# Value products of two attentions: from two query tiles at a time to four

## The chip, the cores and the metric

The kernel runs on one core of a Trainium2 chip. The metric is the device time of one execution in microseconds (us); of the kernel before there are three such times, and one more execution was taken by the profiler. Lower is better.

## The reference, cut to what matters

Two layers of a bidirectional encoder over 1024 tokens of width 1024, all in float32. Layer 0 is a differential attention with 8 heads (two score matrices a head, and a value width of 128), layer 1 a latent attention with 8 heads (one score matrix a head, value width 128). What the change touches is the last line of each attention block, the product of the probabilities with the values:

```
# layer 0
p = softmax(scores); p = p[:, :, 0] - lam * p[:, :, 1]
o = einsum('bhqk,bkhd->bqhd', p, v)
# layer 1
p = softmax(scores)
o = einsum('bhqk,bkhd->bqhd', p, v)
```

Each head has 1024 queries, 1024 keys and 128 value columns. Before and after the attentions stand the input and output projections, norms and gates.

## The kernel before, in words

**Products in three passes.** An f32 operand is kept as two f32r tiles, a rounded part and the rest, and every product is three matmuls that add up in one PSUM bank (`mm3`, L183 to L186).

**Work of one query tile.** Queries go in tiles of 128, eight to a head. In layer 0 `q_tile` (L763) makes two score tiles of 128x1024 (called c0 and c1 here; four matmuls of 512 columns each). `softmax_part` (L396) takes the negated row maximum on DVE (L399) and the exponential on ACT (L401). The c1 scores are overwritten by their exponentials in PSUM, and the two are combined on DVE (L779 to L781), so the PSUM of c1 comes free only with L781. There are two such PSUM tiles (tag `sc`), used in turn. In layer 1 `scores1` (L1595) makes one score tile with ten matmuls and softmax works on that.

**From scores to output.** A finished tile is a `Tail` (L869). Its `turn(kh)` transposes four 128x128 blocks on TensorE into the one `tr` bank (L382), ACT copies them out as `pth` (L384) and DVE writes the rest `ptl` (L385). Its `pv(kh)` makes 4 x 3 matmuls of a value block with the transposed probabilities, for half of the keys; two calls make the 24 matmuls that one pair of query tiles needs. Two tiles share one set of `pth`/`ptl` (`alloc_pt`, 256 columns), so `pv` does something for every second tile only, with 256 moving columns. The output bank `o_` takes four tiles (one half of the queries); with its second pair it is closed, which starts the norm or gate of that half.

**Order of the work.** `attn0` (L931) and `attn1` (L1618) issue one slot for each query tile: the scores of this tile, `turn(1)` of the tile two back, and then `after_scores` (L914): `turn(0)` of the last tile and `pv` of the tile two back. Between these, `fill(i)` takes some steps of a stream: the input projections (layer 0) or the low-rank expansions (layer 1) that later heads need. A step is one `mm3` of 512 columns into an `acc` bank; eight steps in layer 0 make one half of a strip, whose result goes through rope: an ACT copy, four DMAs, products on POOL and DVE, and DMAs that place the halves of q and k. The tables `FILL0`, `FILL1` and `FILL7` (the last head of layer 0) say how many steps each place of each slot gets. In layer 0 a slot gets 6 steps, in layer 1 two slots get 3 together. Strips bring their weights by DMA (L208), and split them on ACT (L229) and POOL (L230).

**A scheduler** in the language's tile layer then orders the instructions of each engine by its own estimate of what is ready, so the built order can differ from the one written. On SP, where the DMAs are issued, and on the other engines, the order of the built program is kept in the run.

**Values.** The values of a layer are computed in `v0_tile` (L667) and `v1_tile` (L1471), stored to DRAM by `store_v` (L359) and read back for each head by `load_v` (L369) just ahead of that head's first `pv`. Eight of the value tiles of layer 1 use the buffers of `pth` and `ptl` (tag `pt`, six of 128x2x512) before the attention needs these.

Of the kernel before, what the change touches and what calls it, by code (L numbers as in the profile page):

```python
# [12 lines left out]
F32R = mybir.dt.float32r  # L13
# [8 lines left out]
P = 128  # L22
# [63 lines left out]
def trunk(ctx: ExitStack, tc: tile.TileContext, A, out):  # L86
# [96 lines left out]
    def mm3(psum, ah, al, bh, bl, first, last):  # L183
        PE.matmul(psum, ah, bh, start=first, stop=False)  # L184
        PE.matmul(psum, ah, bl, start=False, stop=False)  # L185
        PE.matmul(psum, al, bh, start=False, stop=last)  # L186
# [94 lines left out]
    class Side:  # L281


        def __init__(self):
            self.q = []
# [70 lines left out]
            SP.dma_start(f32v(t[64:128, 0, :]), f32v(t[0:64, 0, :]))  # L356
            SP.dma_start(f32v(t[0:64, 1, :]), f32v(t[64:128, 1, :]))

    def store_v(l, sp, acc, tt, fh, tag="vst", bufs=None):  # L359
        v = sp.tile([P, 2, HF], F32R, name="v_hl", tag=tag, bufs=bufs or VB[l])  # L360
# [16 lines left out]
    def transpose_p(p, pth, ptl, t, kh):  # L377

        tr = bank("tr", "tr", [P, 4, P])
        for j in range(4):  # L380
            kt = kh * 4 + j
            PE.transpose(tr[:, j, :], p[:, kt * P : (kt + 1) * P], ident)  # L382
        dst = slice(t * P, (t + 1) * P)
        mk["S"] = S.copy(pth[kh][:, :, dst], tr).ins  # L384
        mk["V"] = V.tensor_sub(ptl[kh][:, :, dst], tr, f32v(pth[kh][:, :, dst])).ins  # L385
# [483 lines left out]
    class Tail:  # L869


        def __init__(self, qp, t, e, zz, c):
            self.qp, self.t, self.e, self.zz, self.c = qp, t, e, zz, c
            self.mate = tails[1]

        def turn(self, kh):
            if kh == 0:
                self.pt = alloc_pt(self.c["pool"]) if self.t == 0 else self.mate.pt
                self.mate = None
            transpose_p(self.e, *self.pt, self.t, kh)  # L880

        def pv(self, kh):
            c, qp = self.c, self.qp
            if self.t == 0:
                return
            if kh == 0:
                if qp == 0:
                    c["vt"] = load_v(c["pool"], c["l"], c["h"])
                if qp % 2 == 0:
                    c["o_"] = bank("pv", "pv")  # L890
                    c["open"](qp // 2)
            cs = slice((qp % 2) * 256, (qp % 2) * 256 + 256)
            pv(c["o_"][:, cs], c["vt"], *self.pt, kh)
            if kh == 1 and qp % 2 == 1:
                c["close"](qp // 2, c["o_"], self.zz)

    tails, hooks = [None, None], []

    def run_tails(fill):

        prev, last = tails
        prev.turn(1)
        fill(0)
        last.turn(0)
        prev.pv(0)
        prev.pv(1)
        fill(1)
        last.turn(1)
        fill(2)
        last.pv(0)  # L910
        last.pv(1)
        tails[:] = [None, None]

    def after_scores(fill, n):  # L914

        prev, last = tails
        if last:
            last.turn(0)
        fill(n)
        if prev:  # L920
            prev.pv(0)
        fill(n + 1)
        new = hooks[:]
        if prev:
            prev.pv(1)
        fill(n + 2)
        for f in new:
            hooks.remove(f)
            f()

    def attn0(h, fills, extra=None, late=None):  # L931

        def close(half, o_, zz):
            if late and half == 1:
                ctx_["late"] = late(o_, zz)
                return
            o = a0b.tile([P, HF], F32, name="o", tag="o", bufs=2)
            sq = a0b.tile([P, HF], F32, name="osq", tag="osq", bufs=4)
            head_out(o_, o, sq)
            subln(o, sq, zz, half, h, None)  # L940

        ctx_ = dict(pool=a0b, l=0, h=h, open=lambda half: None, close=close)
        for qp in range(4):
            half = qp // 2
            if qp % 2 == 0:
                zz = first.pop(0) if first else sm.tile([P, 4], F32, name="zz")
            for t in range(2):
                fl = fills(qp * 2 + t)

                def fill(i):  # L950
                    if fl[i]:
                        stream0.step(fl[i])

                def mid(c):
                    if c == 0:
                        fill(0)
                        if tails[0]:
# [10 lines left out]
                tails[:] = [tails[1], Tail(qp, t, e0, zz, ctx_)]  # L968
                if extra:
                    extra(qp * 2 + t)  # L970
        if late:
            run_tails(lambda i: extra(8 + i))
            while hooks:
                hooks.pop(0)()
            return ctx_["late"]
# [492 lines left out]
            G.tensor_sub(l_, raw, f32v(h_))  # L1468
            wk[k][fh] = (h_, l_)

    def v1_tile(tt, fh, sp, *buf):  # L1471
# [5 lines left out]
        store_v(1, sp, acc, tt, fh, *buf)  # L1477

    CK, CQ = [[None, None] for _ in range(2)], [[None, None] for _ in range(3)]

# [137 lines left out]
    def attn1(h, fills, extra=None, late=None):  # L1618

        def open_(half):  # L1620
            ctx_["gz"] = wst.tile([P, HF], F32, name="gz1", tag="gz", bufs=3)
            SP.dma_start(ctx_["gz"], zS[h, half])

        def close(half, o_, zz):
            if late and half == 1:
                ctx_["late"] = late(o_, zz, ctx_["gz"])
                return
            o = ap2.tile([P, HF], F32, name="o1", tag="o", bufs=2)
            V.scalar_tensor_tensor(out=o, in0=o_, scalar=0.5, in1=ctx_["gz"], op0=ALU.mult, op1=ALU.mult)
            V.reciprocal(zz, zz)  # L1630
            finish(o, zz, 1, h, half, None, ap2, None)

        ctx_ = dict(pool=ap, l=1, h=h, open=open_, close=close)
        for qp in range(4):
            half = qp // 2
            if qp % 2 == 0:
                zz = first1.pop(0) if first1 else sm.tile([P, 4], F32, name="zz1")
            for t in range(2):
                ti = (qp * 2 + t) % 4
                fl = fills(qp * 2 + t)  # L1640

# [10 lines left out]
                tails[:] = [tails[1], Tail(qp, t, e, zz, ctx_)]  # L1652
                if extra:
                    extra(qp * 2 + t)
        if late:
            run_tails(lambda i: extra(8 + i))
            while hooks:
                hooks.pop(0)()
            return ctx_["late"]

    stream1.step(6)
    v1_left = list(range(NT))
    for n, steps in zip(V1_AT, (steps1[0] - 6, 0)):
        for tt in v1_left[:n]:
            v1_tile(tt, 1, ap, "pt", 6)
        del v1_left[:n]
        stream1.step(steps)
    side.flush()
# [1 line left out]
    zz0 = sm.tile([P, 4], F32, name="zz1")  # L1670
    first1 += [zz0, scores1(0, 0, 0, zz0)]
    for tt in v1_left:
        v1_tile(tt, 1, ap, "pt", 6)
    stv.close()
    ap2 = pool(st5, "attn1b")
    for h in range(NH - 1):
# [166 lines left out]
```

## Time and profile before

| | us |
|---|---|
| median of three executions | 1443.31 |
| lowest and highest | 1442.59 and 1443.35 |
| profiled execution, its own time | 1438.65 |
| its span, first to last instruction | 1436.9 |
| TensorE (PE) busy | 1388.8 |
| PE weight loads busy | 1158.8 |
| VectorE (DVE) busy | 917.5 |
| ScalarE (ACT) busy | 728.7 |
| GpSimd (POOL) busy | 610.6 |

The profiled execution was 4.66 us faster than the median, and 1.75 us of its time lie outside the span. The mean granted clock of TensorE is 0.997.

How to read the rows that follow: a row of a timeline has the start and the duration in us, the engine, the line of the kernel, the operation, output<-inputs, the shape, and a count; in brackets is the idle time of the engine before it and what ended it. A matmul's duration overlaps that of the next, so the cost of one in a dense stream is the distance between two starts. A row of a group has the total busy time and the mean in ns after the bar, and behind the second bar the engine's idle time just before its instructions.

### The profile page before, as it was taken

To read this page: it belongs to the slowest core of one execution; us is meant where nothing else is said; L and a number is where in the kernel's file an instruction comes from. 1 tells how busy PE (TensorE), PEld (TensorE's weight loads), DVE (VectorE), ACT (ScalarE), POOL (GpSimd) and SP (SyncE) were. 2 spreads that over 40 slices of the span, in tenths; PEclk is the share of its full clock that TensorE was granted. 3 is DMA by queue.
4 is the path that set the end of the run, shared out by engine and by line. 5 is a ranking of instruction groups with operands and counts; after the bars stand their busy time and mean duration, and the time that the engine had idled before them with its cause. 6 is when DMAs were issued, how large, how long until landed. Compare 5 with 4: busy or idle time off the path is not lost. (4 is left out here: it accounts for less than half of the span.)

```text
span 1436.9 us, 20644 instructions
## 1 busy us (share of the span) xinstructions
PE 1388.8 (97%) x7388; PEld 1158.8 (81%) x7388; DVE 917.5 (64%) x1372; ACT 728.7 (51%) x1287; POOL 610.6 (42%) x483
## 2 busy tenths in 40 slices
PE   5999999999999999998999999999999999999997
PEld 4778788888888888887787877887888888888886
DVE  6656877767777767677435985545666555555355
ACT  5622375666565656566343452335455554545342
POOL 4416164656464646464461343532141331412572
PEclk9999999999999999999999999999999999999999
DMA  8787723333332333237653145398343432336563
GB/s 326 238 254 237 255 70 93 84 104 81 96 101 84 96 89 91 86 96 248 236 183 125 38 132 184 122 305 236 133 130 111 130 101 77 104 96 217 185 237 136
DMA packets 135527, 213.70 MB, mean 149 GB/s; under 512 B 19072, under 2 KB 56064, under 8 KB 135424
## 3 DMA queue, kind: packets, MB, share of 16 engines
q1 hardware_dynamic: 135424, 212.38, 47.1%
q8 instruction: 58, 0.95, 0.3%
q14 instruction: 45, 0.37, 0.1%
HBM read 137.92 MB, written 50.80 MB: 131 GB/s over the span
## 5 line engine op out<-in xcount | busy, mean ns | idle before, releaser
L384 ACT CAST pth<-tr 128x512 fp32r<-128x512 f32 x256 | 150.6, 588 | 284.2 <-PE tr L382 281.9
L399 DVE TENSOR_REDUCE nm<-s 128x1 f32<-128x1024 f32 x192 | 234.1, 1219 | 77.2 <-PE s L773 65.7
L385 DVE TENSOR_TENSOR ptl<-tr,pth 128x512 fp32r<-128x512 f32 x256 | 176.2, 688 | 139.4 <-ACT pth L384 138.9
L230 POOL TENSOR_TENSOR wl<-wraw,wh 128x512 fp32r<-128x512 f32 (+2 forms) x79 | 103.6, 1314 | 205.6 <-ACT wh L229 183.4
L401 ACT ACTIVATE e<-s,nm 128x1024 f32<-128x1024 f32 x128 | 143.7, 1123 | 29.8 <-DVE nm L399 29.2
L382 PE MATMUL tr<-ident,e 128*128 128x128 f32 x1024 | 155.1, 274 | 2.3 <-DVE ptl L385 2.0
L382 PEld LDWEIGHTS tr<-ident,e 128*128 128x128 f32 x1024 | 121.2, 140 | 43.6 <-DVE ptl L385 19.2
L184 PE MATMUL acc<-h0h,wh 128*128 128x512 f32 x360 | 150.1, 417 | 1.9 <-DVE v_hl L362 1.8
L184 PE MATMUL pv<-pth,vt 128*128 128x256 f32 x512 | 147.1, 287 | 0.0
L185 PE MATMUL pv<-ptl,vt 128*128 128x256 f32 x512 | 145.8, 285 | 0.0
L186 PE MATMUL pv<-pth,vt 128*128 128x256 f32 x512 | 144.7, 283 | 0.0
L186 PE MATMUL acc<-h0h,wl 128*128 128x512 f32 x360 | 143.1, 398 | 0.5 <-POOL wl L230 0.5
L185 PE MATMUL acc<-h0l,wh 128*128 128x512 f32 x360 | 142.0, 394 | 0.0
L1013 POOL TENSOR_TENSOR wol<-wor,woh 128x512 fp32r<-128x512 f32 x64 | 85.0, 1351 | 84.7 <-ACT woh L1012 77.2
L185 PEld LDWEIGHTS pv<-ptl,vt 128*128 128x128 f32 x512 | 97.6, 191 | 2.9
L184 PEld LDWEIGHTS pv<-pth,vt 128*128 128x128 f32 x512 | 97.4, 190 | 2.9 <-ACT pth L384 0.2
L186 PEld LDWEIGHTS pv<-pth,vt 128*128 128x128 f32 x512 | 97.6, 191 | 0.1
L326 POOL TENSOR_TENSOR rp_r<-rp_raw,cosT 128x512 f32<-128x512 f32 x38 | 49.8, 1311 | 91.0 <-ACT rp_raw L321 50.8
L331 POOL TENSOR_TENSOR rp_sw<-rp_sw,sinT 128x512 f32<-128x512 f32 x42 | 55.4, 1318 | 74.1 <-DMA rp_sw<-rp_raw 73.9
L773 PE MATMUL s<-ks,qa 128*128 128x512 f32 x256 | 82.6, 404 | 2.8 <-DVE e L781 2.6
L781 DVE SCALAR_TENSOR_TENSOR e<-s,z,e 128x1024 f32<-128x1024 f32 x64 | 82.1, 1283 | 2.1
L773 PE MATMUL s<-ks,qb 128*128 128x512 f32 x256 | 81.1, 395 | 0.0
(590 smaller groups left out, 3335.4 us busy)
## 6 DMA issues: line engine op xcount, KB each, us to landing
ada<-in_ada_ss SPq DMA_DIRECT2D x32, 512.0 KB, 6.0
wraw<-in_w_s SPq DMA_DIRECT2D x64, 256.0 KB, 2.9
vS<-v_hl SPq DMA_DIRECT2D x32, 512.0 KB, 5.9
vt<-vS SPq DMA_DIRECT2D x32, 512.0 KB, 3.7
wor<-in_w_out SPq DMA_DIRECT2D x64, 256.0 KB, 3.9
rp_sw<-rp_raw SPq DMA_DIRECT2D x168, 64.0 KB, 2.0
bc_s<-bc_d SPq DMA_DIRECT2D x34, 256.0 KB, 4.1
oS<-bc_s SPq DMA_DIRECT2D x30, 256.0 KB, 2.5
```

The lines of the kernel that those rows point to most:

```text
L184: PE.matmul(psum, ah, bh, start=first, stop=False)
L185: PE.matmul(psum, ah, bl, start=False, stop=False)
L186: PE.matmul(psum, al, bh, start=False, stop=last)
L230: sub = (V if pair_of else G).tensor_sub(l_[:, :n], raw[:, :n], f32v(h_[:, :n]))
L382: PE.transpose(tr[:, j, :], p[:, kt * P : (kt + 1) * P], ident)
L384: mk["S"] = S.copy(pth[kh][:, :, dst], tr).ins
L385: mk["V"] = V.tensor_sub(ptl[kh][:, :, dst], tr, f32v(pth[kh][:, :, dst])).ins
L399: mk["V"] = V.reduce_max(nm, s_ps, axis=AX.X, negate=True).ins
L401: mk["S"] = S.activation(e, s_ps, AF.Exp, bias=nm, scale=1.0, accum_out=zs).ins
L773: PE.matmul(s_ps[:, kc * HF : (kc + 1) * HF], src[:, c, ql], KS[h][kc][:, c, :], start=fst, stop=not fst)
L781: combined.append(V.scalar_tensor_tensor(out=e0, in0=e1, scalar=z1[:, 0:1], in1=e0, op0=ALU.mult, op1=ALU.add).ins)
L1013: in_turn(G.tensor_sub(lo, raw, f32v(hi)))
```

## The change

`Tail` now counts tiles 0 to 7 of a head. The transposed probabilities of four tiles (512 columns) go into one set of tiles, and `pv` does its work with the fourth of them: 24 matmuls of 512 columns where there were two times 24 of 256. The second half of the last head of each layer keeps pairs (`pairs`). The tiles of the two key halves have tags of their own (`pt0`, `pt1`), two buffers each, that is one set and no second one: the first tile of the next four can be written when the `pv` of that key half is through. So `pv(0)` now stands ahead of `turn(0)` of the last tile.

The steps of the stream are moved out of the slots with a `pv` (1 and 5): the others get 8 in layer 0 and 2 in layer 1. The sum over a head is the same. The eight value tiles of layer 1 now sit two by two in the four new buffers. Lastly a reserve for DMA descriptors that software writes is set to 1024 bytes, which leaves more of the on-chip memory to the tiles.

```
-FILL0 = ((1, 2, 1, 1, 1, 0), (1, 1, 1, 1, 1, 1)) * 3 + ((1, 2, 1, 1, 1, 0), (1, 1, 1, 1, 1, 0))
-FILL1 = ((1, 0, 1, 0), (0, 1, 0, 0)) * 4
+FILL0 = ((2, 2, 1, 2, 0, 1), (0, 0, 0, 0, 0, 0), (2, 2, 1, 2, 0, 1), (2, 2, 1, 2, 0, 1)) + ((2, 2, 1, 2, 0, 1), (0, 0, 0, 0, 0, 0), (2, 2, 1, 2, 0, 1), (2, 2, 1, 2, 0, 0))
+FILL1 = ((1, 1, 0, 0), (0, 0, 0, 0), (1, 1, 0, 0), (1, 1, 0, 0)) * 2
-FILL7 = ((0, 1, 1, 1, 1, 0),) * 4
+FILL7 = ((1, 1, 1, 2, 0, 0), (0, 0, 0, 0, 0, 0), (1, 1, 1, 2, 0, 0), (1, 1, 1, 3, 0, 0))
...
-    def pv(o_, vt, pth, ptl, kh):
+    def pv(o_, vt, pth, ptl, kh, cs):
         for j in range(4):
-            mm3(o_, vt[kh][:, 0, j, :], vt[kh][:, 1, j, :], pth[kh][:, j, :], ptl[kh][:, j, :], kh + j == 0, kh * 4 + j == NT - 1)
+            mm3(o_[:, cs], vt[kh][:, 0, j, :], vt[kh][:, 1, j, :], pth[kh][:, j, cs], ptl[kh][:, j, cs], kh + j == 0, kh * 4 + j == NT - 1)
...
-    def alloc_pt(ap_):
-        pth = [ap_.tile([P, 4, 2 * P], F32R, name="pth", tag="pt", bufs=6) for _ in range(2)]
-        ptl = [ap_.tile([P, 4, 2 * P], F32R, name="ptl", tag="pt", bufs=6) for _ in range(2)]
-        return pth, ptl
+    def pt_tile(ap_, kh, name):
+        return ap_.tile([P, 4, HF], F32R, name=name, tag=f"pt{kh}", bufs=2)
...
     class Tail:
         def turn(self, kh):
-            if kh == 0:
-                self.pt = alloc_pt(self.c["pool"]) if self.t == 0 else self.mate.pt
-                self.mate = None
-            transpose_p(self.e, *self.pt, self.t, kh)
+            if self.i == 0:
+                for parts, name in zip(self.pt, ("pth", "ptl")):
+                    parts[kh] = pt_tile(self.c["pool"], kh, name)
+            transpose_p(self.e, *self.pt, self.i, kh)
+        def due(self):
+            return self.i == 3 or (self.pairs and self.i == 1)
...
     def after_scores(fill, n):
         prev, last = tails
+        if prev:
+            prev.pv(0)
         if last:
             last.turn(0)
         fill(n)
-        if prev:
-            prev.pv(0)
         fill(n + 1)
...
+    def v1_home(tt):
+        if tt % 2 == 0:
+            v1_bufs.append(pt_tile(ap, (tt // 2) % 2, "v_hl"))
+        return v1_bufs[-1][:, tt % 2 * 2 : tt % 2 * 2 + 2, :]
...
-    nc = bacc.Bacc("TRN2", target_bir_lowering=False, num_devices=1)
+    nc = bacc.Bacc("TRN2", target_bir_lowering=False, num_devices=1, dynamic_dma_scratch_size=1024)
```

More of the change, by code (lines that the diff above doesn't have):

```diff
@@ L357, in stack_q, with store_v @@
             SP.dma_start(f32v(t[0:64, 1, :]), f32v(t[64:128, 1, :]))
-    def store_v(l, sp, acc, tt, fh, tag="vst", bufs=None):
-        v = sp.tile([P, 2, HF], F32R, name="v_hl", tag=tag, bufs=bufs or VB[l])
+    def store_v(l, sp, acc, tt, fh, tag="vst", bufs=None, v=None):
+        if v is None:
+            v = sp.tile([P, 2, HF], F32R, name="v_hl", tag=tag, bufs=bufs or VB[l])
         S.copy(v[:, 0, :], acc)
@@ L904, in run_tails @@
         last.turn(0)
-        prev.pv(0)
-        prev.pv(1)
         fill(1)
@@ L967, in attn0 @@
                 side.tick()
-                tails[:] = [tails[1], Tail(qp, t, e0, zz, ctx_)]
+                tails[:] = [tails[1], Tail(qp * 2 + t, e0, zz, ctx_, bool(late) and half == 1)]
                 if extra:
@@ L1469, in load_wk, with v1_tile @@
             wk[k][fh] = (h_, l_)
-    def v1_tile(tt, fh, sp, *buf):
+    def v1_tile(tt, fh, sp, *buf, home=None):
         acc = bank("acc", "vps")
@@ L1476, in v1_tile @@
             mm3(acc, ch[:, c_], cl[:, c_], wk[k][fh][0], wk[k][fh][1], k == 0, k == 1)
-        store_v(1, sp, acc, tt, fh, *buf)
+        store_v(1, sp, acc, tt, fh, *buf, v=home)
     CK, CQ = [[None, None] for _ in range(2)], [[None, None] for _ in range(3)]
@@ L1651, in attn1 @@
                     after_scores(fill, 1)
-                tails[:] = [tails[1], Tail(qp, t, e, zz, ctx_)]
+                tails[:] = [tails[1], Tail(qp * 2 + t, e, zz, ctx_, bool(late) and half == 1)]
                 if extra:
@@ L1659, in attn1 @@
             return ctx_["late"]
+    v1_bufs = []
+    def v1_home(tt):
+        if tt % 2 == 0:
+            v1_bufs.append(pt_tile(ap, (tt // 2) % 2, "v_hl"))
+        return v1_bufs[-1][:, tt % 2 * 2 : tt % 2 * 2 + 2, :]
     stream1.step(6)
@@ L1664, in trunk @@
         for tt in v1_left[:n]:
-            v1_tile(tt, 1, ap, "pt", 6)
+            v1_tile(tt, 1, ap, home=v1_home(tt))
         del v1_left[:n]
@@ L1672, in trunk @@
     for tt in v1_left:
-        v1_tile(tt, 1, ap, "pt", 6)
+        v1_tile(tt, 1, ap, home=v1_home(tt))
     stv.close()
```

29 lines of the change are left out of this document (16 added, 13 removed).

## Prediction

> **What bounds the kernel now.** I read the page first, then who waited for whom on PE, then the busy time of each engine by stage, then the timeline.
>
> ```profile
> span 1436.9 us, 20644 instructions
> ...
> PE 1388.8 (97%) x7388; PEld 1158.8 (81%) x7388; DVE 917.5 (64%) x1372; ACT 728.7 (51%) x1287; POOL 610.6 (42%) x483
> ```
> ```profile
> 200.00:630.00 430.00, 428.76 (x2394) 363.28 (x2393) 306.73 (x439) 261.25 (x461) 239.61 (x199) 1.00 0.32 92
> ...
> 1030.00:1345.00 315.00, 315.00 (x1923) 270.96 (x1922) 179.93 (x256) 165.36 (x299) 92.84 (x72) 1.00 0.40 121
> ```
> ```profile
> PE s L773 <- DVE e L781: 2.6, 4, 0.9
> ...
> PE tr L382 <- DVE ptl L385: 2.0, 4, 0.7
> ```
>
> In the two attention stretches (layer 0 from 200 to 630, layer 1 from 1030 to 1345) PE is busy 428.76 of 430 and 315.00 of 315 us, at a granted clock of 1.00 (third column from the right); DVE, next, is busy 306.73 and 179.93. The two waits an attention could cause, for a score bank and for the transpose bank, come to 2.6 and 2.0 us in all. So the bound is the stream of matmuls, and its length is what counts: the distance between starts.
>
> **The wide product.** The page gives the counts:
>
> ```profile
> L184 PE MATMUL pv<-pth,vt 128*128 128x256 f32 x512 | 147.1, 287 | 0.0
> ```
>
> Three such groups make 1536 products. In the built order of the changed kernel there are 720 of 512 columns and 96 of 256 (the second half of both last heads): 1440 narrow ones become 720 wide ones, 360 in each layer. The mean of 287 ns is no price, since rows overlap; the distance is. First runs of narrow products, two of layer 0 (12 products from 399.71 to the `acc` row, 12 from 401.85) and one of layer 1 (23 from 1100.61 to the score row):
>
> ```profile
> 399.71 0.28 PE L184 MATMUL pv<-pth,vt 128*128 128x256 f32 x1
> ...
> 401.15 0.39 PE L184 MATMUL acc<-h0h,wh 128*128 128x512 f32 x1
> ...
> 401.85 0.28 PE L184 MATMUL pv<-pth,vt 128*128 128x256 f32 x1
> ...
> 403.27 0.39 PE L184 MATMUL acc<-h0h,wh 128*128 128x512 f32 x1
> ...
> 405.61 0.27 PE L382 MATMUL tr<-ident,e 128*128 128x128 f32 x1
> ```
> ```profile
> 1100.61 0.28 PE L185 MATMUL pv<-ptl,vt 128*128 128x256 f32 x1
> ...
> 1103.37 0.39 PE L1611 MATMUL s<-kn_h,qn_h 128*128 128x512 f32 x1
> ```
>
> That is 1.44/12 = 0.120, 1.42/12 = 0.118 and 2.76/23 = 0.120 us. Now 512 columns, between transposes: layer 0, 10 products from 403.27 to 405.61 above and 12 from 358.49 to 361.28; layer 1, 8 from 1107.50 to 1109.34; and for the fastest, 34 distances of the output projection:
>
> ```profile
> 358.49 0.39 PE L185 MATMUL acc<-h0l,wh 128*128 128x512 f32 x1
> ...
> 361.28 0.38 PE L382 MATMUL tr<-ident,e 128*128 128x128 f32 x2
> ```
> ```profile
> 1107.50 0.39 PE L185 MATMUL acc<-ckl,wh 128*128 128x512 f32 x1
> ...
> 1109.34 0.60 PE L382 MATMUL tr<-ident,e 128*128 128x128 f32 x4
> ```
> ```profile
> 692.03 0.40 PE L185 MATMUL oacc<-wol,oth 128*128 128x512 f32 x1
> ...
> 699.76 0.39 PE L186 MATMUL oacc<-woh,otl 128*128 128x512 f32 x1
> ```
>
> They give 2.34/10 = 0.234, 2.79/12 = 0.2325, 1.84/8 = 0.230 and 7.73/34 = 0.2274 us. A wide product streams the same columns as two narrow ones and saves one product's fixed part. Layer 0: 2 x 0.1192 - 0.2325 = 0.0059, times 360, is 2.1 us. Layer 1: 2 x 0.120 - 0.230 = 0.010, times 360, is 3.6 us. I take **5.7 us** of gain. Bounds: the slowest wide against the fastest narrow rate (0.2367 - 0.234 = 0.0027, times 720) is 1.9; the fastest wide against 0.240 (0.0126 x 720) is 9.1.
>
> The Trainium skill, page "TensorE: Matmul & The Clock Gate", section "Back-to-back issue gap", has another price: on a warm array an isolated product takes its columns at 2.4 GHz and about 2.5 ns. By it the saving is 720 x 2.5 ns = 1.8 us; the rows above, with 10 and more ns beyond the columns' time, speak against it here.
>
> **Slots with a `pv` and no fill.** In layer 0, slots 1 and 5 lose their 6 steps. The risk is the c1 bank: c1 of one slot can start only when L781 of the slot before is through. A slot of head 3, as it is:
>
> ```profile
> 356.18 0.63 PE L773 MATMUL s<-ks,qa 128*128 128x512 f32 x2
> ...
> 357.31 1.22 DVE L399 TENSOR_REDUCE nm<-s 128x1 f32<-128x1024 f32 x1 [0.79 <-PE s L773]
> ...
> 358.93 1.10 ACT L401 ACTIVATE s<-s,nm 128x1024 f32<-128x1024 f32 x1
> ...
> 360.68 1.28 DVE L781 SCALAR_TENSOR_TENSOR e<-s,z,e 128x1024 f32<-128x1024 f32 x1
> ...
> 362.41 0.63 PE L773 MATMUL s<-ks,qa 128*128 128x512 f32 x2
> ```
>
> From the start of c1 to the end of L781 are 360.68 + 1.28 - 356.18 = 5.78 us; the next c1 starts 0.45 us later, so PE did not wait. In the built order of the changed kernel the work between these two starts, from slot 0 to 1, is 4 score products, 3 and 9 stream products, 4 of c0, two groups of transposes and N products of `pv`, which the scheduler put ahead of c1, N from 1 to 8. A transpose group costs 0.45 (0.36 from its start to the next, and 0.09 that the next takes longer, as the starts 357.81, 358.17 and 358.49 in the same timeline show). That is 20 x 0.2325 + 0.90 = 5.55, and 0.2325 N: 5.78 with N = 1, 6.5 with N = 4. It just reaches. The chain may stretch to 6.54 us, the distance of two c1 starts where both waited for L781:
>
> ```profile
> 657.02 0.73 PE L773 MATMUL s<-ks,qa 128*128 128x512 f32 x2 [0.92 <-DVE e L781]
> ...
> 663.56 0.73 PE L773 MATMUL s<-ks,qa 128*128 128x512 f32 x2 [0.67 <-DVE e L781]
> ```
>
> There are 15 such slots (slot 5 of 8 heads, slot 1 of 7). I take 0.3 us in all; bounds 0 and 15 x (6.54 - 5.78) = 11.4. In layer 1 DVE does one maximum a slot and no L781, and slot 1 has ten score products and 24 of `pv`; I take nothing there.
>
> **The first head of layer 0** has no earlier head's `pv`. Before, slot 3 has a `pv`; after, the first is in slot 5, and slot 1 has no steps. The c1 starts of its tiles 2, 3 and 4 are now:
>
> ```profile
> 171.24 0.62 PE L773 MATMUL s<-ks,qa 128*128 128x512 f32 x2
> ...
> 177.99 0.62 PE L773 MATMUL s<-ks,qa 128*128 128x512 f32 x2
> ...
> 186.46 0.63 PE L773 MATMUL s<-ks,qa 128*128 128x512 f32 x2
> ```
>
> After, the built order has 18 products and 2 groups, then 20 and 3, between them: 5.1 and 6.0 us, against a chain of 6.54: 1.4 + 0.5 = 1.9 us idle. Before, the same count gives 6.6 and 8.06 in distances of 6.75 and 8.47: 0.6. The difference is **1.4 us** lost; bounds 0 and 4.
>
> **The last head of layer 0.** The `pv` of slot 3 moves to slot 5, and slots 4 and 6 have no steps in either kernel. From c1 to c1 over tiles 3 to 6 the built order after holds 3.7, 5.3 and 6.4 us of work, before 5.4, 4.3 and 5.4; short of 6.54 by 4.1 and by 4.4 us. Nothing; bounds -1 and +2.
>
> **Steps, strips and queues.** The steps that leave slots 1 and 5 take along their weight DMAs, casts (ACT) and subtractions (POOL), rope copies and DMAs, by at most a slot. The tight place is the start of a head, which needs q of its first half. For the last head:
>
> ```profile
> 624.72 0.46 SPq L357 DMA_DIRECT2D qb<-qb  x1
> ...
> 627.95 0.63 PE L773 MATMUL s<-ks,qa 128*128 128x512 f32 x2
> ```
> ```profile
> vS<-v_hl SPq DMA_DIRECT2D x32, 512.0 KB, 5.9
> ...
> qb<-qb SPq DMA_DIRECT2D x32, 128.0 KB, 2.3
> ```
>
> The last copy is issued at 624.72 and lands about 2.3 later, at 627.0, 0.9 ahead of its use. After, q's strip ends later: eight steps a slot instead of six, but none in slot 5. In the built order of the last head's start the scheduler has put 18 stream products ahead of the scores, so PE has work; their cover is missing later in slot 1, where `pv` stands. I take nothing; if q is late all the same, 1 to 2 us at each of the last three heads, so up to +5.
>
> New waits: the ACT copy of the first tile of four waits for `pv` of its key half. The transposes it copies stand behind that `pv` on PE, so it waits for PE anyway, and nothing else is held up. At the start of layer 1 the copies wait for the stores of the value tiles (5.9 us to landing); the built order has 36 products of 512 columns, 8.3 us, between the first two transposes. I take 0.5 us here, 0 to 3. ACT, DVE, POOL and DMA otherwise do the same work; the reserve's size moves addresses only.
>
> **The sum.** -5.7 + 0.3 + 1.4 + 0.5 = -3.5 us against the profiled execution's 1438.65, that is 1435.15. That execution was 4.66 below the median of the runs, so for the median 1443.31 - 3.5 = **1439.8 us**.
>
> **Rivals.**
> - *The wide product saves next to nothing* (this also stands for: the change doesn't do what it says). If the fixed part were 2.7 ns, as in the window around 402 us, the gain is 1.9 and is eaten by the 2.2 of losses: 1443.6. For it: layer 0's rows. Against: 0.010 in layer 1. The skill's rule named above would end here too, at 1.8 of gain.
> - *The softmax chain takes the place of the matmuls* in the 15 slots of layer 0. For it: 5.78 of cover against 5.78 of chain, nothing to spare. Price up to 11.4; at 10 it is 1439.8 + 10 = 1449.8, slower. It decides from (5.7 - 1.9) / 15 = 0.25 us a slot on. Against: the scheduler has moved up to 8 products ahead where its estimate was late, and in the kernel before, with as little to spare (0.45 us), only 2.6 us of such waits arose.
> - *All wide at 0.2274 and no new stall*: -9.1 + 1.4, 1435.6.
>
> **How the numbers follow.** Forecast 0.42, no saving 0.30, chain 0.18, fast 0.10. About 0.2%, 2.9 us, is what a measurement of this kernel can tell from no change. Faster than that: 0.33 of the forecast's, the fast case's 0.10 and 0.02 of no saving: 0.45. Slower: 0.17 of the chain's and 0.04 of no saving: 0.21. Within: 0.34. The forecast's own range is 1436 to 1443; the range to hold 8 in 10 reaches from the fast case to the middle of the chain's losses, 1434.5 to 1448.
>
> **What would show it.** Right: distances of 0.230 to 0.233 in the runs of wide `pv`; no bracket on c1 scores beside them; idle PE only near 170 to 185 us. Wrong: `pv` distances near 0.239 (no saving); rows `s L773 <- DVE e L781` many times over 4, or waits of `s` for q at the starts of heads 4 to 7.

## The result, and the profile after

The changed kernel takes 1464.73 us (median of four executions, 1463.11 to 1468.44); the kernel before, beside it, 1442.95. The ratio is 1.0158, 95% interval 1.0135 to 1.0181: 1.6% slower. The prediction was 1439.8 with a range to 1448. The profiled execution took 1465.53 us, with a span of 1463.7.

The page of the changed kernel, its span, the engines and one of the three groups of value products:

```profile
span 1463.7 us, 19218 instructions
...
PE 1393.5 (95%) x6668; PEld 1125.8 (77%) x6668; DVE 925.5 (63%) x1372; ACT 726.0 (50%) x1287; POOL 612.2 (42%) x483
...
L184 PE MATMUL pv<-pth,vt 128*128 128x512 f32 (+1 forms) x272 | 107.4, 395 | 1.1 <-ACT pth L385 1.0
```

The products are there as written: 3 x 272 = 816, that is 720 wide and 96 narrow. They also run at the forecast distance. Two runs of twelve, one of each layer (a row is start, duration, engine, line, operation):

```profile
270.50 0.39 PE L185 MATMUL pv<-ptl,vt 128*128 128x512 f32 x1
...
272.81 0.39 PE L186 MATMUL pv<-pth,vt 128*128 128x512 f32 x1
...
273.04 0.62 PE L772 MATMUL s<-ks,qa 128*128 128x512 f32 x2
```
```profile
1124.44 0.39 PE L184 MATMUL pv<-pth,vt 128*128 128x512 f32 x1
...
1126.96 0.39 PE L186 MATMUL pv<-pth,vt 128*128 128x512 f32 x1
```

2.54/11 = 0.231 and 2.52/11 = 0.229 us. (The first run begins one product earlier, at 270.18, behind a group of transposes, and that first distance is 0.32; the prediction counts it with the transposes.) Over all runs of three or more, without such first distances and without the stretches at half clock, the means are 0.2303 and 0.2297. The products did their part, and the time was lost elsewhere. By the start of the first score and of the last value product, layer 0's attention grew from 538.6 to 562.7 us, by 24.1; layer 1's from 371.8 to 372.4; everything else by 2.2. So the loss is in layer 0. Its whole attention as one window, before and after (PE busy, then the other engines; third column from the right is the granted clock of TensorE):

```profile
153.00:692.00 539.00, 531.50 (x2970) 448.44 (x2969) 392.16 (x563) 326.37 (x576) 281.28 (x233) 1.00 0.36 107
```
```profile
155.00:718.00 563.00, 535.37 (x2610) 432.32 (x2609) 397.89 (x564) 325.34 (x575) 283.50 (x233) 0.99 0.36 102
```

PE stood idle for 7.5 us of the first and 27.6 of the second: 20.1 more. And although it had a little less to do, it was busy 3.9 us longer. Who kept it waiting in that window of the changed kernel (in all, times, longest):

```profile
PE s L772 <- DVE e L780: 8.0, 9, 2.6
PE s L772 <- DMA qa<-qa: 6.8, 5, 4.0
PE tr L383 <- DVE ptl L386: 5.8, 7, 2.0
PE s L772 <- ACT e L400: 2.3, 2, 1.5
```

Before, over the whole run, the first row stood at 2.6 and the third at 2.0; a wait for q did not occur. The longest is at the start of head 4. PE, then the DMA queue of SP:

```profile
434.28 0.39 PE L186 MATMUL acc<-h0h,wl 128*128 128x512 f32 x1
438.66 1.19 PE L772 MATMUL s<-ks,qa 128*128 128x512 f32 x2 [4.00 <-DMA qa<-qa]
```
```profile
432.71 0.32 SPq L408 DMA_DIRECT2D bc_s<-bc_d  x1
433.12 0.38 SPq L208 DMA_DIRECT2D wraw<-in_w_s  x1
433.61 0.50 SPq L356 DMA_DIRECT2D qa<-qa  x1
...
436.15 2.44 SPq L325 DMA_DIRECT2D rp_sw<-rp_raw  x4
```

The copies of q were issued behind a norm's broadcast and a weight load on the same queue, at 433.61, when PE had 1 us of work left. They were slow as well: the four landed 4.5 to 4.9 us after their issue, where the median of the 56 copies of q in layer 0 is 2.3, and the DMA engines were busy 0.93 to 0.98 of each microsecond from 435 to 438. In the changed kernel 13 of the 56 took over 4 us, in the kernel before one. A copy of 2.3 us would have made the wait of 4.00 us some 2.6 us shorter (an estimate from these rows). The second cost is what comes after such a wait, in windows of four us:

```profile
432.00:436.00 4.00, 2.66 (x12) 1.88 (x10) 2.32 (x4) 1.49 (x3) 3.17 (x3) 1.00 0.41 121
436.00:440.00 4.00, 1.34 (x3) 1.05 (x4) 0.00 (x0) 0.00 (x0) 0.00 (x0) 0.63 0.85 205
440.00:444.00 4.00, 4.00 (x13) 3.26 (x12) 1.82 (x2) 1.18 (x2) 2.80 (x2) 0.52 0.00 1
444.00:448.00 4.00, 4.00 (x21) 3.31 (x20) 3.67 (x8) 3.74 (x7) 0.00 (x0) 1.00 0.00 0
```

PE is busy all through 440 to 444 but starts 13 matmuls, where the next window has 21: the clock was granted at 0.52. Summed over windows of 2 us from 154 to 714, busy time multiplied by one minus the clock, this cost 5.9 us in the changed kernel and nothing in the one before. With the 20.1 us of idle time, and less the 2 to 3 us that the products save in layer 0, that makes the 24.1.

### The profile page after: what moved, and what is told of

The parts are those of the page before. It is cut to its first block, busy times and chain, and to the rows that moved or that the text cites. A ratio compares the mean times of both kernels' runs of the same rounds, so it can differ in the third digit from the quotient of the medians.

```text
span 1463.7 us, 19218 instructions
## 1 busy us (share of the span) xinstructions
PE 1393.5 (95%) x6668; PEld 1125.8 (77%) x6668; DVE 925.5 (63%) x1372; ACT 726.0 (50%) x1287; POOL 612.2 (42%) x483
## 5 line engine op out<-in xcount | busy, mean ns | idle before, releaser
L184 PE MATMUL pv<-pth,vt 128*128 128x512 f32 (+1 forms) x272 | 107.4, 395 | 1.1 <-ACT pth L385 1.0
L185 PE MATMUL pv<-ptl,vt 128*128 128x512 f32 (+1 forms) x272 | 104.5, 384 | 0.0
L186 PE MATMUL pv<-pth,vt 128*128 128x512 f32 (+1 forms) x272 | 103.9, 382 | 0.0
L331 POOL TENSOR_TENSOR rp_sw<-rp_sw,sinT 128x512 f32<-128x512 f32 x42 | 56.0, 1333 | 88.4 <-DMA rp_sw<-rp_raw 85.8
L780 DVE SCALAR_TENSOR_TENSOR e<-s,z,e 128x1024 f32<-128x1024 f32 x64 | 82.1, 1283 | 1.8
L184 PEld LDWEIGHTS acc<-h0h,wh 128*128 128x128 f32 x360 | 67.9, 189 | 16.1 <-DVE v_hl L363 3.1
L186 PEld LDWEIGHTS acc<-h0h,wl 128*128 128x128 f32 x360 | 67.7, 188 | 15.3 <-POOL wl L230 0.7
L185 PEld LDWEIGHTS acc<-h0l,wh 128*128 128x128 f32 x360 | 68.2, 189 | 12.1
```

## The experiments

The two theories at the start. **Theory A**: the moved steps cost the time (the tables). **Theory B**: the wide products cost it (four tiles go through one set of buffers, and 24 products stand in one lump). Times are medians; each is compared with the kernel before by ratio, since that one's median moved between 1439.1 and 1442.95. The last two columns come from one profiled execution of each kernel, so differences of 2 or 3 us in them say little by themselves: e15, no different from the kernel before by its ratio, has 541.7 us of layer 0 against 538.6.

| kernel | us | ratio to before, 95% interval | layer 0 attention, us | lost to the clock, us |
|---|---|---|---|---|
| before | 1439.1 to 1442.95 | 1 | 538.6 | 0.0 |
| changed | 1464.73 | 1.0158 (1.0135 to 1.0181) | 562.7 | 5.9 |
| e1 tables only | 1461.14 | 1.0141 (1.0118 to 1.0164) | 558.1 | 7.4 |
| e2 wide, old tables | 1451.57 | 1.0074 (1.0059 to 1.0089) | 551.5 | 4.5 |
| e3 wide in layer 1 only | 1440.88 | 1.0005 (0.9991 to 1.0018) | 539.0 | 0.0 |
| e4 DEF 5 | 1465.91 | 1.0172 (1.0153 to 1.0190) | 558.0 | 1.7 |
| e5 three steps in pv slots | 1453.99 | 1.0099 (1.0082 to 1.0116) | 549.2 | 3.4 |
| e6 ROT 5, DEF 9, ticks | 1456.26 | 1.0111 (1.0090 to 1.0132) | 556.0 | 3.0 |
| e7 FILL0 of before | 1448.27 | 1.0055 (1.0040 to 1.0070) | 547.5 | 0.0 |
| e8 e3, one POOL subtraction free | 1437.84 | 0.9987 (0.9978 to 0.9996) | 538.0 | 0.0 |
| e9 eight weight buffers | 1463.86 | 1.0157 (1.0133 to 1.0181) | 563.6 | 7.6 |
| e10 e1 with the lags of e6 | 1451.70 | 1.0077 (1.0057 to 1.0097) | 548.1 | 1.6 |
| e11 ticks only | 1467.52 | 1.0187 (1.0167 to 1.0208) | 560.8 | 3.2 |
| e12 lump in two | 1444.20 | 1.0031 (1.0018 to 1.0045) | 543.2 | 0.0 |
| e13 e12, lags, and e8's edit | 1443.00 | 0.9999 (0.9986 to 1.0012) | 542.1 | 1.3 |
| e14 ROT 5, DEF 9 only | 1457.71 | 1.0108 (1.0084 to 1.0132) | 554.9 | 4.8 |
| e15 before, ROT 5, DEF 9 | 1443.17 | 0.9996 (0.9980 to 1.0012) | 541.7 | 1.6 |

**e1, the tables alone.** The kernel before with the three lines `FILL0`, `FILL1`, `FILL7` of the change.

> The kernel before (value products of 256 columns, two query tiles at a time) with the three step tables of the changed kernel. Theory A, the moved steps cost the time in layer 0 (q and k of the next head come later, slots without steps leave the softmax chain bare): 1455 to 1468 us, waits of s for the DMA of qa at head starts (5 or so, up to 4 us) as in the changed kernel. Theory B, the loss comes from the wide products themselves (the four tiles' transposes and copies go through one set of buffers, 24 products in one lump): 1442 to 1447 us, no waits for qa.

1461.14 us: Theory A by the time. Between the profiled executions (spans 1464.8 and 1436.9) 19.5 us of the loss lie in layer 0's attention and 3.9 in layer 1's. The waits in layer 0's attention, and the clock around 428 us, behind the shortest of the three for qb:

```profile
PE s L773 <- DMA qb<-qb: 7.2, 3, 2.8
PE s L773 <- DVE e L781: 4.5, 6, 1.4
PE tr L382 <- DVE ptl L385: 2.0, 4, 0.7
...
PE s L773 <- DMA qa<-qa: 1.2, 2, 0.8
```
```profile
424.00:428.00 4.00, 2.12 (x15) 1.63 (x13) 1.08 (x2) 0.00 (x0) 1.06 (x1) 1.00 0.76 211
428.00:432.00 4.00, 4.00 (x13) 3.29 (x14) 1.52 (x2) 1.73 (x3) 2.69 (x2) 0.59 0.09 19
```

Without one wide product, the tables make q late by 8.4 us in all, and the clock takes 7.4 more.

**e2, the wide products with the old tables.** The same three lines, exchanged in the other kernel.

> The changed kernel with the three step tables of the kernel before: steps stay in the slots that have value products. Theory A (moved steps): 1439 to 1445 us, no waits for qa, layer 0 within 3 us of before. Theory B (wide products themselves): 1458 to 1466 us, with the waits of the transposes for ptl and of the scores for e still there.

1451.57: between the two theories. There is one wait for q, of 0.8 us. But layer 0 lost 9.3 of its 12.9 us in its last head (3.0 of them are products that the change moves there from the first head, 24 wide for 72 narrow ones), where the old `FILL7` gives four steps to a slot and the lump leaves slot 3 without a value product; there two waits of s for e take 4.5 us and the clock 4.5. Another 6.0 us were lost in heads 1 to 6, which e7 takes up. So the wide products cost time without any moved step, but less than the moved steps do (e1).

**e3, wide in layer 1 only.** `Tail(..., bool(late) and half == 1)` becomes `Tail(..., True)` in `attn0`, and `FILL0`, `FILL7` are the old ones.

> The changed kernel, but layer 0 with 256 columns again (all heads in pairs) and the step tables of before in layer 0; layer 1 wide with its new table. Layer 0 keeps the new buffers and the new place of the first half of the value products. Both theories: layer 0 as before within 3 us if the buffers are harmless. Layer 1 alone by the distances: 360 x (2 x 0.120 - 0.230) = 3.6 us less, by the stages of the changed kernel's trace about 0.6 more: so 1439.5 if the distances are all, 1443 to 1445 if layer 1 gives its gain back in waits.

1440.88, no difference: the buffers and the new place of `pv(0)` are harmless in layer 0 (539.0 against 538.6), and layer 1 gives its gain back (372.5 us against 371.8).

**e8, that wait of layer 1 taken away.** One row of e3 names the giver, and POOL's timeline the reason:

```profile
1075.47 0.50 PE L186 MATMUL acc<-ckh,wl 128*128 128x512 f32 x1 [2.80 <-POOL wl L230]
```
```profile
1068.19 1.30 POOL L331 TENSOR_TENSOR rp_sw<-rp_sw,sinT 128x512 f32<-128x512 f32 x1 [1.65 <-DMA rp_sw<-rp_raw]
1069.44 1.29 POOL L816 TENSOR_TENSOR o<-o,bc_s 128x512 fp32r<-128x512 f32 x1
1072.01 1.27 POOL L353 TENSOR_TENSOR qpb<-rp_r,qpa 64x512 fp32r<-64x512 f32 x1 [1.28 <-ACT qpa L351]
1073.35 1.26 POOL L354 TENSOR_TENSOR qpb<-rp_r,qpa 64x512 fp32r<-64x512 f32 x1
1074.69 0.72 POOL L230 TENSOR_TENSOR wl<-wraw,wh 128x256 fp32r<-128x256 f32 x1
```

The subtraction that makes `wl` needs 0.72 us, and ACT had made its input by 1067.5. It stood in POOL's order behind a rope product that waited for a DMA, a product on `o`, and two on `qpb`, the first of which waited for ACT.

```
-        if not pair_of:
+        if not pair_of and not l1_on:
             in_turn(sub)
```

(`l1_on` is set at the start of layer 1's attention; in the built order this moves that one instruction ahead of L331 and changes nothing else on POOL.)

> The kernel that is wide in layer 1 alone (e3), with one instruction on POOL moved: the subtraction of a strip's low part in layer 1 is no longer kept in program order, and the one that PE waited 2.8 us for in head 2 goes ahead of a rope product that waits for a DMA and of two stackings of q that wait for ACT. Theory: the wide products of layer 1 do gain, and that wait ate it: no wait for wl in layer 1, its stage from first score to last value product 2.3 us shorter than before (371.83), 1437.5 to 1438.5 us. Rival: another wait comes in its place, 1440 to 1442 us.

1437.84, ratio 0.9987 (0.9978 to 0.9996): the only version here that beats the kernel before, by 0.13%. The interval only just leaves out 1, and of 15 versions one may do that by chance; the gain in layer 1 is firmer, as that stage repeats from profile to profile (371.8 and 371.7 us before and in e15, 370.7 and 371.0 in e8 and e13). The subtraction now starts at 1065.72, and the wait is gone; of its 2.8 us, 1.2 came back as a wait of a transpose for ptl, so layer 1's attention is 370.7 us, 1.1 below before and not 2.3. In heads 3 to 5, where no wait is named in either kernel, 139.14 became 137.83 us: 0.44 a head, which is what the distances said (3.6/8 = 0.45).

**e4, the stacking sooner.** `DEF = 5`.

> The changed kernel with DEF 5 in place of 7: the stacking of k and q follows two steps sooner after the rope, so that fewer of these steps fall behind a slot without any. Theory A1 (q of the next head late, 6.8 us of waits, and the clock that falls after a wait of 4 us, 2 to 4 us more): 1454 to 1458 us and no wait for qa over 1 us. Rival A2 (the waits for qa only stand in for another wait, or the loss is spread over the slots): 1462 to 1466 us.

1465.91, as Rival A2 said: Theory A1's sum is refuted. The waits for q did go (0.4 and 1.5 us are left), and the clock gave back 4.2, but others came:

```profile
PE tr L383 <- DVE ptl L386: 7.6, 8, 1.9
PE s L772 <- DVE e L780: 4.9, 8, 1.0
PE acc L186 <- POOL wl L230: 4.6, 4, 2.1
PE tr L383 <- DVE z L778: 2.5, 1, 2.5
```

POOL's wait for the rope copies, too, was longer (48.5 us from 155 to 660 us, where the changed kernel has 38.0). Layer 0 is 4.7 us shorter in this profile, and the rest of the kernel 3.7 longer. DVE's rope sum (L335), which stands ahead of softmax work in DVE's order, waited 22.6 us for POOL's rope product from 155 to 700 us, where it waited 7.2 in the changed kernel. So q is one end of a chain that is late as a whole.

**e5, half way.** Three steps in the slots with value products, seven in the others.

> The changed kernel with FILL0 half way: 7 steps in three of four slots and 3 in the slots with value products (in place of 8 and 0; 6 and 6 before). Theory C, the loss grows with how unevenly the steps lie (the lags of rope and stacking are counted in steps, and a dense slot gives them less time while an empty one gives q none): half or less of the loss of heads 1 to 6 of layer 0, so 1449 to 1454 us. Rival R1, it is the slot without a step that costs (any steps in it cure it): 1443 to 1447 us. Rival R2, the wide products cost it whatever the table: 1460 to 1465 us.

1453.99, at the upper end of Theory C's range. For heads 1 to 6 of layer 0 the loss goes with the unevenness: 5.8 us with 6 and 6 steps (e7), 11.5 with 7 and 3, 21.3 with 8 and 0 (1.4 and 2.8 us of the last two are stream products that slid into these heads from the first and the last). It does not go to nothing with even steps; e7 says more.

**e6, e11 and e14, the lags.** A rope's product and its stacking follow the strip by ROT and DEF steps. e6 has both edits, e11 the second, by which a slot without steps counts as six for these lags, e14 the first:

```
-ROT = 3
-DEF = 7
+ROT = 5
+DEF = 9
...
                         stream0.step(fl[i])
+                    elif not any(fl):
+                        side.tick()
```

> The changed kernel, its step tables kept, but the lags of rope and stacking put nearer to time: ROT 5 and DEF 9 in place of 3 and 7, and the slots without steps count six places as steps for these lags. Theory C: POOL no longer waits for the rope copies by DMA with the weights' subtraction queued behind it, and q is not held up over the empty slot: idle PE in layer 0's attention from 29.7 us to under 20, 1450 to 1456 us. Rival R3, the lags are not the cause (weights that come late because their buffers are freed late, or the bare softmax chain): 1462 to 1467 us.

> The changed kernel where a slot without steps counts six for the lags (ROT and DEF as they were). It parts the two edits of e6 (1456.3 us). If what matters is q held up over the empty slot: 6.8 us of waits for qa gone, 1454 to 1458 us. If it is the rope product that waits for its DMAs on POOL in the dense slots: near 1463 us.

> The changed kernel with ROT 5 and DEF 9 and no ticks for slots without steps: the other half of e6 (1456.3 us; the ticks alone, e11, gave nothing). If the rope product's wait for its DMAs is what holds POOL, DVE and ACT up in the dense slots: 1454 to 1459 us, POOL's waits for rp_sw from 38 to under 20 us. If only both together help: 1462 us or more, with q late by 2 steps more.

1456.26, 1467.52 and 1457.71: by the ratios e6 and e14 give some 7 us back and e11 none, so they come from ROT and DEF. e6 stays just above Theory C's range, and PE's idle time in its layer 0 is 23.2 us, not under 20. That the empty slot holds q up is refuted: with that slot counted, e11 still waits 8.2 us for qa. POOL's wait for the rope copies from 155 to 660 us, in the kernel before, the changed one and e6:

```profile
POOL rp_sw L331 <- DMA rp_sw<-rp_raw: 27.7, 14, 4.8
```
```profile
POOL rp_sw L331 <- DMA rp_sw<-rp_raw: 38.0, 17, 5.6
```
```profile
POOL rp_sw L331 <- DMA rp_sw<-rp_raw: 11.6, 5, 3.8
```

In a dense slot (eight steps) three steps can pass in 2.1 us (nine products of 0.23 with nothing between), less than the issue of the four rope DMAs alone, 2.44 us in the last of the rows of SP above. e6 removes most of that wait and 5.6 of the 6.8 us of waits for qa; the waits for DVE's e (8.0) and ptl (5.0) stay, and those for ACT's e grow from 2.3 to 5.6. In e14 POOL's wait is down to 4.4 us, so that wait is worth these 7 us and not the rest of the loss.

**e9, more weight buffers.** `bufs=6` becomes 8 for `whl`.

> The changed kernel with 8 buffers in place of 6 for the strips' split weights (two raw blocks more ahead), nothing else. Theory R3, weights late: the weight DMA no longer stands on SP waiting for a buffer in front of the copies of q (3.4 us at the start of head 4), waits for wl and qa fall to under 2 us in layer 0: 1453 to 1458 us. Theory C (lags): nothing, 1462 to 1467 us, since raw buffers and the order on POOL are what they were.

1463.86: Theory R3 is refuted; waits for qa are 5.6 us.

**e10, the lags in e1.**

> The kernel with narrow products and the new tables (e1), with ROT 5, DEF 9 and six ticks for a slot without steps. Theory C (lags counted in steps): the 8.4 us of waits for q and most of the 7.4 us of lost clock after them go, 1446 to 1452 us from 1461. Rival: the dense slots themselves (eight steps' weights, casts and rope in one slot) cost it, 1457 to 1463 us.

1451.70: by the ratios some 9 of the 20 us, at the upper edge of the theory. The waits for q fall from 8.4 to 2.2 us and the clock's part from 7.4 to 1.6; no copy of q takes over 4 us to land any more, where five did in e1. What stays in layer 0 is 9.5 us: the 1.6, and waits of PE that are 7 us longer than before, 2.9 of them for e, 2.2 for q and 1.4 for ptl.

**e15, the control.** The kernel before with ROT 5, DEF 9.

> Control: the kernel before with ROT 5 and DEF 9. If the lags matter only where steps are dense: 1438 to 1443 us, no difference. If longer lags are better whatever the table: 1436 us or less. If later q costs it: 1444 us or more.

1443.17, ratio 0.9996: with even steps the lags make no difference, although POOL's wait for the rope copies, 27.7 us before, is gone from its list. They matter where steps are dense.

**e7, FILL0 of before.**

> The changed kernel with FILL0 of before alone (heads 0 to 6 of layer 0 six steps a slot); FILL7, FILL1 and the wide products as changed. By the stages of the traces so far: heads 0 to 6 as in the kernel with all old tables (+3.6 us), the last head as in the changed one (+0.2), layer 1 as in the changed one (+0.7), input phase about 0: 1440.8 + 4.5 = 1445 us. If the lateness in heads 5 and 7 with the old tables came from the wide products as such and not from FILL7, 1450 us.

1448.27, against 1445 forecast and 1450 by its rival, so nearer to the rival. Heads 0 to 6 came out about as forecast (+2.9 us for +3.6); the last head lost 6.1 us and not 0.2, so its time in the changed kernel did not carry over to other neighbours.

Heads 1 to 6 show what the wide products cost by themselves. They hold the same work in e7 and e2 as before, and took 5.8 and 6.0 us longer, with PE idle for 9.1 us in each, against 1.2; with narrow products and the same new buffers they took 0.4 us longer (e3) and 0.3 us less (e8). So with even steps the wide products save 2.3 us there (288 x 0.0079) and make PE wait some 8 us more, in e7 as s for e (5.7, the larger ones but one at c1 of slots 1 and 5) and as tr for ptl (2.1).

**e12 and e13, the lump in two.** In layer 0 the second 12 products of four tiles move on to the next slot, ahead of the transposes that need their buffers, and the steps are 7, 5, 5, 7 (5, 3, 3, 5 in the last head). e13 adds ROT 5, DEF 9 and e8's edit.

```
+        if prev and prev.c["l"] == 0 and not prev.pairs and prev.i == 3:
+            carry.append(prev)
+        elif prev:
             prev.pv(1)
...
                         fill(0)
+                        if carry:
+                            carry.pop().pv(1)
                         if tails[0]:
```

> Wide products in both layers, but in layer 0 the 24 products of four tiles are parted: 12 in slots 1 and 5, 12 in slots 2 and 6, and the steps are 7, 5, 5, 7 in four slots (5, 3, 3, 5 in the last head), so that slots are 7.7 to 9.1 us of products by the distances and none is empty. Theory F, the loss of layer 0 is uneven slots, of products (softmax chain and DVE bare) with the old table or of steps with the new: waits of s for e and of tr for ptl fall to under 5 us in layer 0, 1441 to 1445 us. Rival W, wide products cost layer 0 as such (one set of buffers, four tiles before the first product): 1448 us or more.

> e12 (wide in both layers, layer 0's value products parted over two slots, steps 7, 5, 5, 7) with ROT 5 and DEF 9 and with the freed subtraction of e8 in layer 1. Theory: the one gives 3 us in layer 1 as it did from e3 to e8, the other takes the POOL waits for rope DMAs out of layer 0, whose waits of s and tr fall from 14 us to about 9: 1437 to 1440 us. Rival W, the rest of layer 0's loss is the four-tile products as such: 1441 to 1443 us.

1444.20 and 1443.00 (1.0031 and 0.9999). Even slots take layer 0 from 562.7 to 543.2 us with its products as wide as in the change, and nothing is lost to the clock; e12 is in Theory F's range. Most of this is the table: e7, with the lump whole, has 547.5, and what e12 gains on it lies in the last head (1.6 us lost for 6.1), while heads 1 to 6 lose as much (5.9, with five more stream products in them). The waits of e12:

```profile
PE s L772 <- DVE e L780: 4.1, 8, 1.3
PE tr L383 <- DVE ptl L386: 4.1, 5, 1.4
PE s L772 <- ACT e L400: 3.1, 2, 1.5
```

The two for e and ptl add up to 8.2, not under 5. e13's gain over e12 is that of layer 1 (371.0 us after 374.0); layer 0 differs by 1.1. By the ratio e13 is no different from the kernel before. Its 1443.00 us is in Rival W's range, its ratio in that of the theory (the kernel before stood at 1439.1 when the range was written and at 1442.84 beside e13), so this run does not choose between them. Layer 0 of e13 is 3.5 us longer than before and 0.4 longer than that of e15, with narrow products and the same lags: what the wide products still cost there is not shown.

## Why the prediction was wrong, step by step

**The wide product: right.** Forecast 5.7 us, from distances of 0.2325 and 0.230; measured 0.2303 and 0.2297 against narrow ones of 0.119 and 0.120 (0.1191 and 0.1197 over all runs), so 360 x 0.0079 + 360 x 0.0097 = 6.3 us. The rival that it saves next to nothing is out. The price of the Trainium skill (page "TensorE: Matmul & The Clock Gate", section "Back-to-back issue gap"), 1.8 us, is out too: 7.9 and 9.7 ns a product were measured, not 2.5.

**"Steps, strips and queues", taken at nothing, at most +5: this step failed.** The moved steps measured 20.4 us by themselves (e1), and the old `FILL0` alone, put back, takes some 15 of the changed kernel's 22 us away (e7). The step looked for the tight place at the right point, q at the start of a head, and named 1 to 2 us at the last three heads; e1 has 1.9 to 2.8 us at three heads, and the changed kernel 4.0 at head 4. But it let PE's 18 products ahead stand for cover, and took 2.3 us for a copy to land, where those that PE waited longest for took 3.9 to 5.3. It counted that the side work of a step moves by at most a slot, and not that its rate rises by a third in the three slots that take eight steps, while its lags are counted in steps: POOL then meets the rope copies before they land, and holds up what stands behind it in its order. Lags two steps longer take this away and give back some 7 us of 22 in the changed kernel (e14) and 9 of 20 in e1 (e10), where most of the waits for q and of the clock lost after them go. For the rest the place of the steps is the cause (e1, e5, e7); how it gets to PE is shown by rows for single waits only, the copies of q above and the rope's sum on DVE below. The rows of the kernel before already held this: 14 waits of POOL for rp_sw, 27.7 us in all, that cost PE nothing as long as slots were even (e15).

**A term that was missing: the clock.** 5.9 us, and 7.4 in e1. The sum priced a wait at its length.

**The slots with a `pv` and no fill, 0.3 us, bounds to 11.4.** Waits of s for e rose from 2.6 to 8.0 us over layer 0, by 5.4; some 5.9 of the 8.0 stand at c1 of slots 1 and 5. That is within the bounds and a good part of the price of the rival that the softmax chain takes over; e2 has such waits without any moved step. The largest is in head 0. PE, then DVE:

```profile
193.93 0.40 PE L184 MATMUL pv<-pth,vt 128*128 128x512 f32 x1
196.90 0.73 PE L772 MATMUL s<-ks,qa 128*128 128x512 f32 x2 [2.57 <-DVE e L780]
```
```profile
194.45 0.69 DVE L335 TENSOR_TENSOR rp_r<-rp_r,rp_sw 128x512 f32<-128x512 f32 x1 [2.38 <-POOL rp_sw L331]
```

The scheduler had put four products of `pv` ahead of c1, the N = 4 of the prediction, and the cover was there: from the c1 before, at 187.62, PE had 6.7 us of work. But the chain took 9.2 us (L780 ended at 196.84) where the prediction has 5.78 to 6.54. The tile's softmax steps stand behind the rope's sum in DVE's order, and DVE stood 2.38 us there for POOL's rope product. The prediction took that chain's length from tiles without such a wait. The same kind of wait is in the group rows of L335 in the last section: 1.9 us in all before, 7.2 in the changed kernel.

**The first head, +1.4, bounds to 4: too small.** It took 66.2 us for 63.5, although 3.0 us of value products had moved from it to the last head (72 narrow ones before, 24 wide after): 5.7 us lost, the 2.57 above among them, and part of it to the clock right after that row:

```profile
198.00:202.00 4.00, 4.00 (x14) 3.13 (x13) 2.66 (x5) 2.42 (x5) 1.78 (x2) 0.57 0.00 0
```

**The start of layer 1, +0.5:** no wait for the stores is named in its head 0. **Layer 1 as a whole** was to gain 3.6 and came out at +0.5: 2.8 of these 4.1 us are one wait behind POOL's order (e3, e8), and for the other 1.3 no row names a wait.

What stays open: e10 and e6 still lose some 10 and 17 us in layer 0 with the new tables. Their rows name DVE's e and ptl, e6's also ACT's e; DVE's wait at the rope's sum is one way that leads there (8.2 us in e6, 3.3 in e10, from 155 to 700 us), but a kernel with that sum moved was not tried. Nor was a copy of q that does not share the DMA engines with a broadcast and a weight load.

## What to carry to other kernels

When steps of a side stream are moved, price the rate and not only the sum: count what every engine and queue that serves a step must do in the densest slots, and check each lag that is counted in steps against the time of the DMA that it has to cover. Where PE is the bound, a wait can cost its length and again as much in the clock. When a copy is what PE will wait for, look at what is issued just ahead of it: its time to land is not a constant. A gain of 10 ns a product is soon eaten: try the parts of a change one by one (here layer 1 by itself came out even, and slightly ahead once one instruction on POOL was moved).

## What the runs showed of the hardware

**The clock can fall after a wait of under 2 us, and need not after a longer one.** In e1 one bracketed wait was followed by the clock of 0.59 shown above; in e4 a longer one was not. The two rows, and the windows around that of e4:

```profile
427.95 0.70 PE L773 MATMUL s<-ks,qb 128*128 128x512 f32 x2 [1.88 <-DMA qb<-qb]
```
```profile
486.38 0.63 PE L383 MATMUL tr<-ident,e 128*128 128x128 f32 x4 [2.48 <-DVE z L778]
```
```profile
483.00:487.00 4.00, 1.51 (x9) 1.04 (x9) 3.03 (x5) 1.73 (x4) 2.66 (x3) 1.00 0.17 66
487.00:491.00 4.00, 4.00 (x20) 3.24 (x19) 2.25 (x3) 1.87 (x3) 1.99 (x2) 1.00 0.02 4
```

So 1.88 us of waiting was enough in one place, and 2.48 not in the other. The Trainium skill, page "TensorE: Matmul & The Clock Gate", section "HAM oscillation — how this bites in real kernels", says to have no gaps over about 3.4 us; by that rule only the wait of 4.00 us, of those quoted here, would have cost clock, and the 1.88 us above speak against it.

The traces show what decides beside the length. In each of the 17, every stretch at half clock begins a whole number of times 3.413 us after the first one, and all but a run's last are one or two such cells long (3.41 or 6.83 us). The wait of e1 lies within one cell of this grid (425.28 to 428.69, PE busy for 1.53 of 3.41 us), and the next cell ran at 0.50. The wait of e4 is parted between two (481.94 to 485.35, busy 1.96; 485.35 to 488.76, busy 2.38), and no half clock followed. Over all 17 traces, from 60 us on and without the last 8, each of the 39 full-clock cells with PE busy under 44% was followed by half clock, 21 of the 183 between 44 and 70%, and none of the 6564 above. Part 1 of the same page of the Trainium skill calls the window in which activity is counted free-running; the traces agree, as the grid lies differently in each run (e1's begins at 53.23 us, e4's at 51.85). So the same wait can cost clock in one execution and not in another: that for `wl` in layer 1 was 2.8 us in e3 and e12, and head 2 of layer 1 took 48.1 us in the one and 49.7 in the other, which lost a cell's half.

**One DVE addition takes 0.68 or up to 2.05 us.** The rope's last sum (L335, both inputs in SBUF), 28 times in layer 0's attention, as a group before and after (behind the bar the total in us and the mean in ns):

```profile
L335 DVE TENSOR_TENSOR rp_r<-rp_r,rp_sw 128x512 f32<-128x512 f32 x28 | 22.2, 794 | 1.9 <-POOL rp_sw L331 1.9
```
```profile
L335 DVE TENSOR_TENSOR rp_r<-rp_r,rp_sw 128x512 f32<-128x512 f32 x28 | 30.1, 1074 | 7.5 <-POOL rp_sw L331 7.2
```

Before, 2 of the 28 took over 1.4 us, after, 8; most took 0.68. One of the slow ones, on DVE, and POOL beside it:

```profile
328.80 1.76 DVE L335 TENSOR_TENSOR rp_r<-rp_r,rp_sw 128x512 f32<-128x512 f32 x1 [1.65 <-POOL rp_sw L331]
```
```profile
328.72 1.29 POOL L230 TENSOR_TENSOR wl<-wraw,wh 128x512 fp32r<-128x512 f32 x1
329.97 2.00 POOL L810 TENSOR_TENSOR o<-o,bc_s 128x512 f32<-128x512 f32 x1
```

The addition began while POOL was in a subtraction, and POOL's next product in turn took 2.00 us, where the mean of its line is 1.58. All 15 additions over 0.9 us, of the 56 in the two kernels, began inside an instruction of POOL and ended 0.55 us after it; none that found POOL idle took over 0.70. At 335.04 PE waited 2.00 us for a transpose bank behind that stretch. The Trainium skill, page "SBUF — State Buffer", section "Who interferes with whom", has a DVE instruction with two SBUF inputs contend with a GpSimd one that reads SBUF, the first to issue blocking the other; these rows agree. That DVE's 7.9 us more here are a cause of the waits for ptl was only argued from the order of the rows, not tried; the `ptl` that PE waited for at 335.04 had itself waited 1.38 us for ACT's `pth`.
